# A row-sum stream on one core: two buffers of 24 rows in place of three of 16

## The chip, the core and the metric

The kernel runs on one core of a Trainium2 chip. The metric is the device time of one execution in microseconds (us); several runs are summarised by their median.

## The reference

```python
def setup_inputs():
    batch, seq, dim = 32, 512, 1024
    return {"x": np.random.randn(batch, seq, dim).astype(np.float32), "divisor": float(dim)}

def reference(x, divisor):
    return (np.sum(x, axis=-1) / divisor).astype(np.float32)
```

There are 16,384 rows of 1,024 float32 values. Each row is summed and divided by 1,024. The input has 67.1 MB, the output 64 KB.

## The kernel before, in words

Each of the 128 partitions is given J = 128 rows. They lie in three regions of `x`: the first F = 15 rows of each partition (`x_first`, where partitions are 15 rows apart), then M = 97 rows (`x_main`) and L = 16 rows (`x_last`), which share a region where partitions are W = M + L = 113 rows apart. The rows of one partition that one load fetches are contiguous in memory, so a load of 16 rows moves one run of 64 KB for each partition, 8 MB in all.

The loads go through three buffers, `bulk0` to `bulk2`, of 16 rows per partition each, used in turn. Their list is written by hand: from the main region 2 rows, five times 16, and 15; then the 15 rows of the first region; then two loads from the last region, of 10 rows and 640 elements and of 3 rows and 672 elements. Two small loads with places of their own (`pa`, `pb`) bring what is left of the last region, 1,344 and 416 elements per partition. The text counts the loads through the buffers from 0. Each buffer has a semaphore that its loads raise by 16 on landing.

All loads are issued by SP (SyncE) on one queue. The first two go out before anything else. The loop at L134 issues the others in order. Load 2 waits for load 0 to land. Each later load k waits until load k-3, which had the same buffer, has been reduced: `done_dve` and `done_act` hold the counts that the semaphores of DVE and ACT must reach. Behind the loop SP issues `pa` and `pb`, then the store of the first region's results (after POOL has scaled them), the store of the main region's, and last the store of `fin`, the results of the last region.

DVE (VectorE) takes one `reduce_sum` per load (L215). Of some loads it leaves the last rows to ACT, which sums a row per instruction (L183): the second number in each pair of the list says how many, 4 of the 15 in the last main load and 6 of the 15 in the first region's. POOL scales the results of these two regions (L157, L161). The rows of the last region are summed by DVE with an instruction that adds the two halves of a row (L205) and by ACT, both of which scale at once; the order of these is written so that little is left after the last bytes.

A change to the list of loads, to the number of buffers or to their size thus moves the landings, the reductions and the time at which SP may issue.

Of the kernel before, what the change touches and what calls it, by code (L numbers as in the profile page):

```python
# [35 lines left out]
def kernel(  # L36
# [6 lines left out]
    nc = tc.nc  # L43
    nc.at_finalize(start_loads_at_once)
    xf = x.flatten_outer_dims()
    N, D = xf.shape
# [2 lines left out]
    J = N // P  # L49
    assert J * P == N  # L50

    F, L = 15, 16
    M = J - F - L
    W = M + L
    x_first = bass.AP(tensor=x.tensor, offset=0, ap=[[F * D, P], [1, F * D]])
# [1 line left out]
    x_last = bass.AP(tensor=x.tensor, offset=P * F * D + M * D, ap=[[W * D, P], [1, L * D]])  # L57
# [4 lines left out]
    def room(name, *shape):  # L62
        return nc.alloc_sbuf_tensor(name, [P, *shape], F32).ap()
# [2 lines left out]
    base = -(-nc.sbuf_base // 32) * 32  # L66
    room("pad", -base % 1024 // 4)
    assert nc.sbuf_base % 1024 == 0
    bulk = [room(f"bulk{i}", 16 * D) for i in range(3)]

# [2 lines left out]
    ends = [0, 10 * D + c10, 14 * D + c14, 15 * D + c15, 16 * D]  # L75
# [11 lines left out]
    loads = []  # L87
    sems = {}

    def sem(name):  # L90
        sems[name] = nc.alloc_semaphore(name)
        return sems[name]

    in_bulk = [sem(f"in_bulk{i}") for i in range(3)]
    in_pa, in_pb = (sem(f"in_{n}") for n in ("pa", "pb"))
    out_first, out_main = sem("out_first"), sem("out_main")
    dve, act, pool = sem("by_dve"), sem("by_act"), sem("by_pool")
    done = sem("done")
    landed = nc.alloc_semaphore("landed")

    main = [(2, 0)] + [(16, 0)] * 5 + [(15, 4)]
    first = [(15, 6)]
    assert sum(r for r, _ in first) == F and sum(r for r, _ in main) == M
    for rows_of, src, dst in ((main, x_main, res), (first, x_first, res0)):
        j = 0
        for rows, on_act in rows_of:
            t = bulk[len(loads) % 3][:, : rows * D]
            loads.append((t, in_bulk[len(loads) % 3], src[:, j * D : (j + rows) * D], on_act, dst[:, j : j + rows]))
            j += rows
    for k in range(2):  # L110
        t = bulk[len(loads) % 3][:, : ends[k + 1] - ends[k]]
        loads.append((t, in_bulk[len(loads) % 3], x_last[:, ends[k] : ends[k + 1]], 0, None))


    for t, s, src, *_ in loads[:2]:
        i = nc.sync.dma_start(out=t, in_=src).then_inc(s, 16)
        tc.no_tile_sem_insts.add(i.ins.name)
    tc.close()
    tc.compile()  # L119
# [2 lines left out]
    done_dve, done_act = {}, {}  # L122
# [4 lines left out]
    arrived, seen = [], {}  # L127
# [6 lines left out]
    for k, (t, s, src, *_) in enumerate(loads):  # L134
        if k < 2:
            continue
        if k == 2:
            nc.sync.wait_ge(loads[0][1], arrived[0])
        else:
            nc.sync.wait_ge(dve, done_dve[k - 3])  # L140
            if done_act[k - 3]:
                nc.sync.wait_ge(act, done_act[k - 3])
            nc.sync.wait_ge(s, arrived[k] - 16)
        nc.sync.dma_start(out=t, in_=src).then_inc(s, 16)
    nc.sync.dma_start(out=pa, in_=x_last[:, ends[2] : ends[3]]).then_inc(in_pa, 16)
    nc.sync.dma_start(out=pb[:, : D - c15], in_=x_last[:, ends[3] : ends[4]]).then_inc(in_pb, 16)
    nc.sync.wait_ge(pool, 3)
# [6 lines left out]
    k = len(main) - 1  # L154
# [31 lines left out]
    for k, (t, s, src, on_act, dst) in enumerate(loads[:-2]):  # L186
        rows = t.shape[1] // D
# [23 lines left out]
    for k, (t, s, src, on_act, dst) in enumerate(loads[:-2]):  # L211
        m = t.shape[1] // D - on_act
        nc.vector.wait_ge(s, arrived[k])
        rows = t[:, : m * D].rearrange("p (r d) -> p r d", d=D)
# [65 lines left out]
```

## Time and profile before

| | us |
|---|---|
| median of 3 runs | 160.44 |
| lowest, highest | 160.27, 160.67 |
| span of the profiled execution, from its first to its last instruction | 159.3 |
| DVE busy in it | 116.7 |
| ACT busy in it | 18.6 |
| a 16-row reduction on DVE | 17.22 |
| a row on ACT | 1.01, and 0.19 to read the sum |

The page gives the span as the profiled execution's own time; the median of the unprofiled runs lies 1.1 us above it, which is the time around the first and last instruction. The DMA queue moved 67.18 MB in 2,160 packets, at 422 GB/s over the span. The time from issue to landing of a load (a median of 40.8 us for the 16-row loads) includes its wait behind earlier loads in the queue.

A line of the timeline has the start and the duration in us, the engine, the line of the kernel, the operation, what it writes and reads, and in brackets the idle time of the engine ahead of it and what ended that. Landing means that the load's semaphore is full. "SPq" is SP's instruction queue, which issues the DMAs.

### The profile page before, as it was taken

What the parts mean: (1) busy time and instruction counts of PE and PEld (TensorE: products, weight loads), DVE (VectorE), ACT (ScalarE), POOL (GpSimd) and SP (SyncE); (2) the same over time, 40 slices, a digit from 0 to 9 for tenths busy, and PEclk for the clock granted to TensorE, in tenths of its full rate; (3) what the DMA queues carried; (4) which work ended last, traced back from release to release, by engine and by line L of the source; (5) the groups of instructions that cost most, each with busy time, mean ns of one, the idle gap of its engine ahead of it and who ended that gap; (6) DMA issues with size and microseconds to landing.
All of it is one profiled execution on the core that took longest, in us unless ns stands there. A gap on an engine that the chain in (4) does not pass through costs nothing.

```text
span 159.3 us, 144 instructions
## 1 busy us (share of the span) xinstructions
DVE 116.7 (73%) x32; ACT 18.6 (12%) x35; POOL 1.0 (1%) x7
## 2 busy tenths in 40 slices
DVE  0500009999499994999949999499989990399296
ACT  3000000000000000000000000000009100392196
POOL 0000000000000000000000000000000001000000
DMA  8996996996996997979969969969996999889894
GB/s 296 494 527 263 527 527 263 527 527 263 527 527 263 527 444 346 527 313 477 527 263 527 527 263 527 494 278 463 494 494 262 478 494 494 350 350 525 344 401 154
DMA packets 2160, 67.18 MB, mean 422 GB/s; under 512 B 624, under 2 KB 752, under 8 KB 880
## 3 DMA queue, kind: packets, MB, share of 16 engines
q1 hardware_dynamic: 2160, 67.18, 98.1%
HBM read 67.11 MB, written 0.07 MB: 422 GB/s over the span
## 4 chain that ended last, share of the span: by engine, by line
DMA 67%; DVE 30%; another core or an unknown queue 1%; issue 0%
DMA bulk<-in_x_dram 67%; DVE res L215 29%; DVE bulk L205 1%; DVE tail L205 0%; DVE pb L205 0%; DVE fin L205 0%
## 5 line engine op out<-in xcount | busy, mean ns | idle before, releaser
L215 DVE TENSOR_REDUCE res<-bulk 128x16 f32<-128x16384 f32 (+3 forms) x8 | 110.0, 13754 | 37.7 <-DMA bulk<-in_x_dram 37.7
L183 ACT ACTIVATE junk<-bulk 128x1024 f32<-128x1024 f32 (+1 forms) x16 | 15.6, 973 | 137.2 <-DMA bulk<-in_x_dram 137.2
L205 DVE CUSTOM_DVE_ANT_0 bulk<-bulk 128x512 f32<-128x512 f32 (+1 forms) x9 | 5.5, 665 | 3.1 <-DMA bulk<-in_x_dram 3.1
L183 ACT ACTIVATION_READ_ACCUMULATOR junk<-bulk 128x1 f32 x16 | 3.0, 187 | 0.0
L183 ACT ACT_TABLE_LOAD x1 | 1.3, 1283 | 1.9 <-PEq L119 1.9
L157 POOL TENSOR_SCALAR res<-res 128x97 f32<-128x97 f32 x1 | 0.5, 465 | 129.8 <-DVE res L215 129.8
L205 DVE DVE_READ_ACCUMULATOR2_ANT fin<- 128x1 f32 x10 | 0.8, 82 | 0.0
L183 ACT ACTIVATE junk<-tail 128x737 f32<-128x737 f32 x1 | 0.8, 789 | 0.0
L205 DVE CUSTOM_DVE_ANT_0 bulk<-bulk,part 128x192 f32<-128x192 f32 x1 | 0.4, 420 | 0.3 <-DMA bulk<-in_x_dram 0.3
L205 DVE CUSTOM_DVE_ANT_0 tail<-tail 128x304 f32<-128x304 f32 x1 | 0.5, 476 | 0.0
L205 DVE CUSTOM_DVE_ANT_0 pb<-pb 128x209 f32<-128x209 f32 x1 | 0.4, 379 | 0.1
L161 POOL TENSOR_SCALAR res<-res 128x15 f32<-128x15 f32 x1 | 0.3, 262 | 15.6 <-DVE res L215 15.6
L183 ACT ACTIVATION_READ_ACCUMULATOR junk<-tail 128x1 f32 x1 | 0.2, 187 | 0.0
L153 POOL MEMSET pb<- 128x2 f32 x1 | 0.1, 99 | 1.5 <-POOLq L119 1.5
L261 POOL MEMSET const-bfloat16-1.0<- 128x1 bf16 x1 | 0.1, 101 | 0.0
L261 POOL MEMSET const-uint8-127<- 128x1 uint8 x1 | 0.1, 101 | 0.0
L261 POOL MEMSET const-float32-0.0<- 128x1 f32 x1 | 0.1, 98 | 0.2 <-issue 0.2
L261 POOL MEMSET const-float32-1.0<- 128x1 f32 x1 | 0.1, 98 | 0.0
L205 DVE DVE_READ_ACCUMULATOR2_ANT pb<- 128x1 f32 x1 | 0.1, 84 | 0.0
L205 DVE DVE_READ_ACCUMULATOR2_ANT part<- 128x1 f32 x1 | 0.1, 83 | 0.0
## 6 DMA issues: line engine op xcount, KB each, us to landing
bulk<-in_x_dram SPq DMA_DIRECT2D x2, 7680.0 KB, 39.3
bulk<-in_x_dram SPq DMA_DIRECT2D x1, 5440.0 KB, 32.0
bulk<-in_x_dram SPq DMA_DIRECT2D x1, 1872.0 KB, 23.5
bulk<-in_x_dram SPq DMA_DIRECT2D x1, 1024.0 KB, 4.6
tail<-in_x_dram SPq DMA_DIRECT2D x1, 672.0 KB, 24.7
pb<-in_x_dram SPq DMA_DIRECT2D x1, 208.0 KB, 24.8
bulk<-in_x_dram SPq DMA_DIRECT2D x5, 40.8
out_dram<-res SPq DMA_DIRECT2D x1, 48.5 KB, 1.6
```

Of the source, the lines that this page charges most:

```text
L153: nc.gpsimd.memset(pb[:, D - c15 :], 0.0).then_inc(pool)
L157: nc.gpsimd.tensor_scalar_mul(out=res, in0=res, scalar1=scale).then_inc(pool)
L161: nc.gpsimd.tensor_scalar_mul(out=res0, in0=res0, scalar1=scale).then_inc(pool)
L183: nc.scalar.activation(scratch, src, COPY, scale=by, accum_out=dst).then_inc(count)
L205: return nc.vector.tensor_tensor_reduce(out=src[:, :h], in0=src[:, :h], in1=src[:, h:], scale=by, scalar=ahead, op0=ADD, op1=ADD, accum_ou ...
L215: nc.vector.reduce_sum(out=dst[:, :m], in_=rows, axis=AX).then_inc(dve)
L261: nc = _bacc.Bacc("TRN2", target_bir_lowering=False, num_devices=1)
```

## The change

The three buffers of 16 rows become two of 24, which take the same room (192 KB per partition). The main region has 98 rows in loads of 2 and four times 24, with 8 rows of the last of them left to ACT; the first region has 14 rows, 5 of them on ACT; the last region's 16 rows, their loads and their arithmetic are as before. Partitions of the main and last regions lie 114 rows apart. A load of 24 rows is written as two runs of 12 rows (48 KB) per partition. Load k now waits for load k-2 to be reduced, and load 2 does so as well, where it waited for load 0's landing. There are eight loads through the buffers (0 to 7) in place of ten (0 to 9): load 4 is the last of the main region, load 5 the first region, loads 6 and 7 the last one.

```diff
-    F, L = 15, 16
+    F, L = 14, 16
...
-    bulk = [room(f"bulk{i}", 16 * D) for i in range(3)]
+    bulk = [room(f"bulk{i}", 24 * D) for i in range(2)]
...
-    in_bulk = [sem(f"in_bulk{i}") for i in range(3)]
+    in_bulk = [sem(f"in_bulk{i}") for i in range(2)]
...
-    main = [(2, 0)] + [(16, 0)] * 5 + [(15, 4)]
-    first = [(15, 6)]
+    main = [(2, 0)] + [(24, 0)] * 3 + [(24, 8)]
+    first = [(14, 5)]
...
-            t = bulk[len(loads) % 3][:, : rows * D]
-            loads.append((t, in_bulk[len(loads) % 3], src[:, j * D : (j + rows) * D], on_act, dst[:, j : j + rows]))
+            t = bulk[len(loads) % 2][:, : rows * D]
+            loads.append((t, in_bulk[len(loads) % 2], src[:, j * D : (j + rows) * D], on_act, dst[:, j : j + rows]))
...
-        t = bulk[len(loads) % 3][:, : ends[k + 1] - ends[k]]
-        loads.append((t, in_bulk[len(loads) % 3], x_last[:, ends[k] : ends[k + 1]], 0, None))
+        t = bulk[len(loads) % 2][:, : ends[k + 1] - ends[k]]
+        loads.append((t, in_bulk[len(loads) % 2], x_last[:, ends[k] : ends[k + 1]], 0, None))
...
+    def load(t, src):
+        if t.shape[1] > 16 * D:
+            t, src = (v.rearrange("p (c f) -> p c f", c=2) for v in (t, src))
+        return nc.sync.dma_start(out=t, in_=src)
...
-        if k == 2:
-            nc.sync.wait_ge(loads[0][1], arrived[0])
-        else:
-            nc.sync.wait_ge(dve, done_dve[k - 3])
-            if done_act[k - 3]:
-                nc.sync.wait_ge(act, done_act[k - 3])
-            nc.sync.wait_ge(s, arrived[k] - 16)
-        nc.sync.dma_start(out=t, in_=src).then_inc(s, 16)
+        nc.sync.wait_ge(dve, done_dve[k - 2])
+        if done_act[k - 2]:
+            nc.sync.wait_ge(act, done_act[k - 2])
+        nc.sync.wait_ge(s, arrived[k] - 16)
+        load(t, src).then_inc(s, 16)
```

More of the change, by code (lines that the diff above doesn't have):

```diff
@@ L106 @@
         for rows, on_act in rows_of:
-            t = bulk[len(loads) % 3][:, : rows * D]
-            loads.append((t, in_bulk[len(loads) % 3], src[:, j * D : (j + rows) * D], on_act, dst[:, j : j + rows]))
+            t = bulk[len(loads) % 2][:, : rows * D]
+            loads.append((t, in_bulk[len(loads) % 2], src[:, j * D : (j + rows) * D], on_act, dst[:, j : j + rows]))
             j += rows
     for k in range(2):
-        t = bulk[len(loads) % 3][:, : ends[k + 1] - ends[k]]
-        loads.append((t, in_bulk[len(loads) % 3], x_last[:, ends[k] : ends[k + 1]], 0, None))
+        t = bulk[len(loads) % 2][:, : ends[k + 1] - ends[k]]
[4 more added lines that the diff above has]
+        return nc.sync.dma_start(out=t, in_=src)
     for t, s, src, *_ in loads[:2]:
-        i = nc.sync.dma_start(out=t, in_=src).then_inc(s, 16)
+        i = load(t, src).then_inc(s, 16)
         tc.no_tile_sem_insts.add(i.ins.name)
```

## The prediction

> **What bounds the kernel now.** I read the page's totals first, then the timeline of DVE and of SP's issues, then the stretches in which the DMA engines fall idle, and the instruction groups by shape for prices.
>
> The totals:
>
> ```profile
> span 159.3 us, 144 instructions
> ...
> DVE 116.7 (73%) x32; ACT 18.6 (12%) x35; POOL 1.0 (1%) x7
> ...
> q1 hardware_dynamic: 2160, 67.18, 98.1%
> ```
>
> The one DMA queue has packets in flight on the 16 engines for 98.1% of the span; DVE, the busiest engine, works for 73%. So the stream of loads sets the time, and compute matters in two ways only: the tail after the last byte, and the moment at which a buffer comes free for the next load. The timeline gives both (start, duration, line, operation, and in brackets the idle time before):
>
> ```profile
> 43.28 17.22 DVE L215 TENSOR_REDUCE res<-bulk 128x16 f32<-128x16384 f32 x1 [2.13 <-DMA bulk<-in_x_dram]
> 62.65 17.22 DVE L215 TENSOR_REDUCE res<-bulk 128x16 f32<-128x16384 f32 x1 [2.15 <-DMA bulk<-in_x_dram]
> ...
> 119.83 11.89 DVE L215 TENSOR_REDUCE res<-bulk 128x11 f32<-128x11264 f32 x1 [1.04 <-DMA bulk<-in_x_dram]
> ...
> 137.99 9.76 DVE L215 TENSOR_REDUCE res<-bulk 128x9 f32<-128x9216 f32 x1 [6.26 <-DMA bulk<-in_x_dram]
> ...
> 150.82 0.49 DVE L205 CUSTOM_DVE_ANT_0 bulk<-bulk 128x320 f32<-128x320 f32 x1 [3.08 <-DMA bulk<-in_x_dram]
> ```
>
> Each reduction starts some 0.02 us after its load has landed, so starts are landings. A 16-row load takes 62.65 - 43.28 = 19.37 us; from the first start (4.61) to that of the fourth 16-row load (81.98) 64 rows take 77.37, which is **1.209 us a row**. DVE needs 17.22 for the same 16 rows and waits 2.1 at each seam. SP's issue of the buffer that has come free, from its own timeline:
>
> ```profile
> 60.53 0.33 SPq L144 DMA_DIRECT2D bulk<-in_x_dram  x1
> ```
>
> At 60.53 one load has 2.1 us left, a whole further load is queued behind it, and this one goes behind both. With three buffers the stream has over 21 us of work ahead whenever SP issues; it cannot run dry.
>
> **The change part by part.**
>
> *DVE's price for other row counts.* The groups by shape:
>
> ```profile
> L215 DVE TENSOR_REDUCE res<-bulk 128x16 f32<-128x16384 f32 x5 | 86.1, 17220 | 25.8 <-DMA bulk<-in_x_dram 25.8
> ...
> L215 DVE TENSOR_REDUCE res<-bulk 128x9 f32<-128x9216 f32 x1 | 9.8, 9755 | 6.3 <-DMA bulk<-in_x_dram 6.3
> ...
> L215 DVE TENSOR_REDUCE res<-bulk 128x2 f32<-128x2048 f32 x1 | 2.3, 2286 | 4.6 <-DMA bulk<-in_x_dram 4.6
> ```
>
> (17.220 - 2.286) / 14 = 1.067 us a row and 0.153 fixed; this gives 9.755 for nine rows, as measured. So 24 rows cost 25.76, and DVE's 16 rows of the last main load 17.22. ACT's eight rows there cost 8 x 1.04 = 8.4 (its 1.01 us ACTIVATEs start 1.04 apart), beside DVE and done 9 us earlier.
>
> *Bytes and packets.* The rows are the same 128. In the packet records a 65,536-byte packet starts 2.4145 us after the one before it on its engine, and a 61,440-byte one 2.2635: both 0.1509 a row, so two 48 KB packets in place of one cost nothing measurable. Two fewer loads remove two completion packets, 0.006 us each on an engine. Sum: 0.
>
> *The start.* Load 0 (2 rows) is alike. The third load now waits for DVE's 2-row reduction and goes at 4.61 + 2.29 = 6.9 instead of 4.60; load 1 (24 rows) covers it until 33.6. What is queued behind that wait on SP is only later loads. Cost 0; without that cover it would be 2.3.
>
> *The 24-row seams.* Now load k+2 is issued when load k is reduced, with only the rest of load k+1 ahead of it. A 24-row load takes 29.0, its predecessor's reduction 25.76: SP issues 3.2 us before the running load lands (loads 3, 4 and 5, at about 59.4, 88.4 and 117.4, against landings at 62.6, 91.6 and 120.6). By the packet records engines finish 0.34 to 0.7 us before the landing, so some 2.5 us are left for the issue to bring its first packet. What that takes, the stretches beside an idle queue show (share of the DMA engines, GB/s in the last two columns):
>
> ```profile
> 0.00:0.90 0.90, 0.00 (x0) 0.00 (x0) 0.19 (x4) 1.00 0.00 0
> 0.90:1.00 0.10, 0.00 (x0) 0.00 (x0) 0.00 (x0) 1.00 0.41 82
> ...
> 158.60:158.70 0.10, 0.00 (x0) 0.00 (x0) 0.00 (x0) 1.00 0.08 9
> ```
>
> The first load, issued at 0.00, has its first packet just before 1.00; the last store, issued at 157.85, at 158.68. So 0.83 to 1.0, against 2.5: hidden, cost 0.
>
> *The seam before the last region.* Here the cover fails. Load 6 (10.6 rows of the last 16) takes the buffer of load 4, which DVE works on for 17.22 from its landing. Ahead of it there is only load 5, the first part, 14 rows long: 14 x 1.209 = 16.93. Load 4 lands at 4.61 + 96 x 1.209 = 120.7 and load 5 at 137.6; DVE is done with load 4 at 137.9, and SP issues load 6 at 137.93 (0.03 after DVE's end, as at 41.15 and 41.18). That is **0.33 after load 5 has landed**: the DMA engines are dry, and every later byte of the stream is late by the gap. Three buffers had this load queued at 118.82, 19 us early.
>
> The gap's size: load 6 lands an empty-queue overhead plus its transfer time after its issue, where before it landed its transfer time after load 5. So the loss is 0.33 plus that overhead. The trace has two rows on an empty queue. The last store (8 KB) lands 1.4 us after its issue, under 0.1 of it packets: 1.3 or more of overhead, a loss of 1.65. Load 0 lands 4.58 after its issue; less 2 x 1.209 that is 2.16, a loss of 2.49. Load 0 is the nearer row, since it is a read of the same tensor, but its first packets took 0.3 to 0.8 us where later ones of that size took 0.309, with a second load issued 0.43 behind it and all engines starting together. I expect part of that slow start and take an overhead of 1.77: **a loss of 2.1**, ends 1.65 and 2.5.
>
> The Trainium skill ("DMA: Bandwidth & Descriptors", section on the anatomy of one DMA) fits a transfer alone as about 2.0 us plus bytes over 436 GB/s, on the GpSimd path; by that estimate load 6 (5.57 MB) needs 14.8 against 12.84 in the trace, a loss of 2.3 rather than 2.1.
>
> *After it.* Load 7 waits for load 5's reduction (nine rows, 137.9 + 9.76 = 147.7, issue then; the two small loads follow on SP by 148.6), and load 6's data run until about 152.3, so the queue stays fed. From load 6's landing on, loads and instructions are those of before: 159.3 - 150.8 = 8.5 us. POOL's scalings and the first store come at 148, idle work.
>
> Sum on the profiled execution: 159.3 + 2.1 = 161.4 of span. The median lies 1.1 above the span (160.44 against 159.3); I keep that: **162.5 us**.
>
> **The rivals.**
>
> 1. *Two buffers suffice* (no change, 160.4). If load 6 were issued 1.3 us before load 5's landing there would be no gap. That needs DVE's 16 rows to take 15.6 where five of them took 17.22 on average. Chance 0.03. The Trainium skill ("Trainium Kernel Development and Optimization", Best Practices) advises double buffering to overlap DMA with compute, and would make this the case; no row here shows a two-deep queue.
>
> 2. *A fixed cost per load, and two loads fewer* (faster). If each load paid the last store's 1.4 on the stream, two fewer would bring -2.8, and with the gap +2.1 the time is 159.7. It decides from 1.05 us per load up. Against it: eight 65,536-byte packets per engine take 8 x 2.4145 = 19.32, and the first four landings are 19.32 to 19.37 apart, so a seam costs under 0.05. Chance 0.03. The fixed 2.0 us named above, if it held per queued DMA, would give -4.0 here; the trace disagrees.
>
> 3. *The 24-row seams fail too* (slower still). A load in two runs a partition is 256 descriptors; nothing in the trace is issued so. Should its first packet need three times the 0.83 to 1.0, it comes up to 0.5 late at loads 3 and 4 (load 5 has one run again): +1.0, 163.5; it decides above 2.5 us. For it: an engine stretched now and then (the fifth 16-row landing came 0.25 late) eats cover. Chance 0.07.
>
> 4. *Slower reads at the new pitch.* 114 rows instead of 113 lie between partitions' reads. The only bad stretch shown, 19.6 for 16 rows instead of 19.35, is 1.3%; over 114 rows 1.8 us, 164.3 with the gap. Against it: undisturbed 61,440-byte packets take 2.267 at the 15-row and at the 113-row pitch alike. Chance 0.03.
>
> A view folded back into one run per partition would leave the last gap as it is, since load 6 has one run anyway.
>
> **How the numbers follow.** The forecast, one gap before the last region, has 0.84. Its own range is 1.65 to 2.5 plus 0.3 either way for stretched packets: 161.8 to 163.2. Reaching to rival 3 (163.5, and some above) gives 161.7 to 163.8, leaving out rivals 1, 2, 4. A measurement of this kernel can tell about 0.3%, 0.5 us, from no change. Faster 0.03 (rival 2), same 0.03 (rival 1), slower 0.94.
>
> **What would show it right or wrong.** Right: DVE's 24-row reductions at 25.8 each, SP's issues about 3.2 before the landings up to load 5; load 6 issued some 0.3 after load 5's landing, next to DVE's end of the 16-row reduction; a stretch of some 1.5 us near 138 without DMA; load 6 landing near 15 us after load 5 instead of 12.8; 8.5 from there to the end. Wrong: no idle DMA at 138 (rivals 1, 2), landings of 24 rows over 29.3 apart with the DMA engines idle at 62 and 91 (rival 3) or with packets over 1.82 us each (rival 4).

## The result and the profile after

The changed kernel takes 164.34 us (median of 5 runs, 163.88 to 164.98) against 160.44: a ratio of 1.0244, 95% interval 1.0232 to 1.0257. That is 3.9 us slower; 2.1 was forecast, and the range ended at 163.8. A later series gave 1.0263 (1.0245 to 1.0282). Ratios, here and below, leave out a run that lay over 1.5% above the fastest of its kernel; two of the experiments had one each. The span of the profiled execution grew from 159.3 to 163.0, 3.7 us.

The totals after:

```profile
span 163.0 us, 145 instructions
...
DVE 113.2 (69%) x30; ACT 21.8 (13%) x41; POOL 1.0 (1%) x7
...
q1 hardware_dynamic: 2384, 67.18, 96.7%
```

The same bytes are moved, but packets are in flight for less of the span, so the time went into a stream that is not fed. DVE's timeline shows where (start, duration, line, operation, idle time before):

```profile
4.82 2.29 DVE L217 TENSOR_REDUCE res<-bulk 128x2 f32<-128x2048 f32 x1 [4.82 <-DMA bulk<-in_x_dram]
33.77 25.75 DVE L217 TENSOR_REDUCE res<-bulk 128x24 f32<-128x24576 f32 x1 [26.67 <-DMA bulk<-in_x_dram]
62.76 25.75 DVE L217 TENSOR_REDUCE res<-bulk 128x24 f32<-128x24576 f32 x1 [3.24 <-DMA bulk<-in_x_dram]
92.00 25.75 DVE L217 TENSOR_REDUCE res<-bulk 128x24 f32<-128x24576 f32 x1 [3.48 <-DMA bulk<-in_x_dram]
...
121.92 17.22 DVE L217 TENSOR_REDUCE res<-bulk 128x16 f32<-128x16384 f32 x1 [4.17 <-DMA bulk<-in_x_dram]
...
139.32 9.75 DVE L217 TENSOR_REDUCE res<-bulk 128x9 f32<-128x9216 f32 x1 [0.19 <-DMA bulk<-in_x_dram]
...
154.49 0.49 DVE L207 CUSTOM_DVE_ANT_0 bulk<-bulk 128x320 f32<-128x320 f32 x1 [5.42 <-DMA bulk<-in_x_dram]
```

The reductions cost what was worked out (25.75 for 24 rows). The landings do not keep their distance: 28.99 from load 1 to load 2, then 29.24 and 29.92 to loads 3 and 4. Load 4 lands at 121.9 instead of 120.7. The next lines are from SP's timeline: the issue of load 5 and of load 6. Behind them stand the stretches around the last issue (columns: stretch, length, busy times of DVE, ACT and POOL, clock, share of the DMA engines, GB/s):

```profile
117.78 0.34 SPq L118 DMA_DIRECT2D bulk<-in_x_dram  x1
...
139.16 0.34 SPq L118 DMA_DIRECT2D bulk<-in_x_dram  x1
```

```profile
136.00:137.00 1.00, 1.00 (x1) 0.00 (x0) 0.00 (x0) 1.00 0.79 344
137.00:137.30 0.30, 0.30 (x1) 0.00 (x0) 0.00 (x0) 1.00 0.00 0
137.30:139.10 1.80, 1.80 (x1) 0.00 (x0) 0.00 (x0) 1.00 0.01 0
```

A packet is counted in the stretch in which it starts, so 0.00 alone is not idleness; the packet records complete it. The engines finish load 5 between 137.5 and 139.0, and load 6 has its first packets at 140.1 to 141.0, so all 16 engines stand still, each for a time between 1.1 and 3.5 us. Load 6 lands 15.3 us after its issue, where its bytes alone take 12.84.

So the forecast gap is there, but it is not the whole loss: the seams between the 24-row loads, costed at nothing, lose time too.

### The profile page after: what moved, and what is told of

Read it like the earlier page. It is cut to its first block, busy times and chain, and to the rows that moved or that the text cites. A ratio compares the mean times of both kernels' runs of the same rounds, so it can differ in the third digit from the quotient of the medians.

```text
span 163.0 us, 145 instructions
## 1 busy us (share of the span) xinstructions
DVE 113.2 (69%) x30; ACT 21.8 (13%) x41; POOL 1.0 (1%) x7
## 4 chain that ended last, share of the span: by engine, by line
DMA 60%; DVE 38%; ACT 1%; issue 1%; SPq 0%
DMA bulk<-in_x_dram 60%; DVE res L217 38%; ACT junk L185 1%; SPq L118 0%
## 5 line engine op out<-in xcount | busy, mean ns | idle before, releaser
L217 DVE TENSOR_REDUCE res<-bulk 128x24 f32<-128x24576 f32 (+3 forms) x6 | 106.5, 17753 | 42.6 <-DMA bulk<-in_x_dram 42.6
L185 ACT ACTIVATE junk<-bulk 128x1024 f32<-128x1024 f32 (+1 forms) x19 | 18.6, 978 | 137.8 <-DMA bulk<-in_x_dram 137.8
L185 ACT ACTIVATION_READ_ACCUMULATOR junk<-bulk 128x1 f32 x19 | 3.5, 187 | 0.0
L159 POOL TENSOR_SCALAR res<-res 128x98 f32<-128x98 f32 x1 | 0.5, 466 | 137.2 <-DVE res L217 137.2
## 6 DMA issues: line engine op xcount, KB each, us to landing
bulk<-in_x_dram SPq DMA_DIRECT2D x1, 5440.0 KB, 15.3
```

Source lines behind the costliest of these rows:

```text
L159: nc.gpsimd.tensor_scalar_mul(out=res, in0=res, scalar1=scale).then_inc(pool)
L185: nc.scalar.activation(scratch, src, COPY, scale=by, accum_out=dst).then_inc(count)
L217: nc.vector.reduce_sum(out=dst[:, :m], in_=rows, axis=AX).then_inc(dve)
```

## Experiments

Below, a load's *lead* is the time from SP's issue of it to the landing of the load ahead of it in the queue. It depends on how many rows DVE keeps: each row given to ACT frees the buffer 1.07 us earlier. In the changed kernel loads 3, 4 and 5 have a lead of 3.2 to 4.1, load 6 of 0.14 and load 7 of 5.4; in the kernel before, the 16-row loads have over 21.

*Theory A:* an issue on a busy stream takes more than the lead to bring all engines their first packets, so some engines run dry, and first packets are stretched. *Rival B:* the form of the loads (two runs per partition) or the new spacing of 114 rows unbalances the engines, whatever the lead. Ratios are to the kernel before on the same chip; "above before" is the ratio applied to the median of before there (160.36 to 160.56).

### Only the last seam closed

```diff
-    main = [(2, 0)] + [(24, 0)] * 3 + [(24, 8)]
+    main = [(2, 0)] + [(24, 0)] * 3 + [(24, 12)]
```

> The changed kernel with ACT taking 12 rows of load 4 instead of 8, so DVE reduces 12 rows (12.95 us) and load 6 is issued about 4 us before load 5 lands instead of 0.14 before it. The prediction's step (the gap before load 6 is the whole loss): about 160.5. Theory A (a load issued only 2 to 3 us ahead of its turn also has its first packets stretched on some engines, here at loads 3, 4 and 5): the gap of 2.3 goes and the rest stays, 161.5 to 162.3. Rival B (the two-run form or the new pitch unbalances the engines): the same 161.5 to 162.3; this run only prices the gap.

Measured: ratio 1.0113 (1.0091 to 1.0136), 1.8 us above before. The gap's removal gives back about 2.1, and nearly as much stays: the gap is not the whole loss. The rest is not the seams alone, though. With load 6 in time, load 7 is issued only 3.1 us before load 6 lands, and in the profile it lands 0.45 late; the next run shows this more strongly. This does not tell A from B.

### Every load early, still two buffers of 24 rows in two runs

```diff
-    main = [(2, 0)] + [(24, 0)] * 3 + [(24, 8)]
+    main = [(2, 0)] + [(24, 6)] * 3 + [(24, 12)]
```

> The changed kernel with ACT taking 6 rows of loads 1 to 3 and 12 of load 4, so that every load is issued 9 us (load 6: 4 us) ahead of the landing of the load before it. Two buffers, 24 rows, two runs and pitch as in the changed kernel. Theory A (late issues stretch first packets): all loss goes, 160.2 to 160.8, landings 29.0 apart, no stretched packets at the seams. Rival B (form or pitch): the seams stay stretched, 161.5 to 162.3.

Measured: 1.0107 (1.0086 to 1.0128), 1.7 above before. That is the time that rival B gave, but not by its way: it had the seams stay stretched, and in the profile loads 0 to 6 are in time (load 6 lands at 150.8, as in the kernel before). The loss lies at load 7, which theory A had not counted. That load has a lead of 3.0 there, since the DVE part of load 5 holds its buffer:

```profile
147.80 0.33 SPq L118 DMA_DIRECT2D bulk<-in_x_dram  x1
```

Packets at its start are stretched by up to 0.99 us, and load 7 lands at 156.25 instead of 155.3. The trouble had moved to the one load whose lead was still 3 us. The next run gives that load a lead as well:

```diff
-    first = [(14, 5)]
+    first = [(14, 7)]
```

> As e2_share, and ACT also takes 7 rows of load 5 instead of 5, so that load 7 is issued 5.2 us before load 6 lands (3.0 in e2_share). Every load is now issued at least 4 us ahead. Theory A (issues 2 to 3 us ahead are late, since the first packets come 2.2 to 3.8 us after the issue when the engines are busy): 160.3 to 160.8, no stretched packets at load 7. Rival B (form or pitch): as e2_share, 161.7 to 162.2.

Measured: 160.91, 1.0021 (1.0012 to 1.0030). Of the 3.9 us, 0.35 are left (theory A's range ended at 160.8, and the kernel before takes 160.56 on this chip). Nothing but the shares of DVE and ACT was changed: two buffers, 24 rows, two runs per partition and the spacing are those of the changed kernel. Rival B falls as the cause of the loss.

```profile
62.92 19.35 DVE L217 TENSOR_REDUCE res<-bulk 128x18 f32<-128x18432 f32 x1 [9.65 <-DMA bulk<-in_x_dram]
92.00 19.35 DVE L217 TENSOR_REDUCE res<-bulk 128x18 f32<-128x18432 f32 x1 [9.72 <-DMA bulk<-in_x_dram]
120.97 12.95 DVE L217 TENSOR_REDUCE res<-bulk 128x12 f32<-128x12288 f32 x1 [9.62 <-DMA bulk<-in_x_dram]
```

Landings are 29.08 and 28.97 apart, as the bytes demand.

### The two terms, each alone, on top of that version

The seams (`main` with `[(24, 0)] * 3 + [(24, 12)]`, `first` with `(14, 7)`):

> As e5_all, but loads 1 to 3 are all on DVE as in the changed kernel: loads 3, 4 and 5 are issued 3.2 us before the running load lands, loads 6 and 7 in good time. The prediction's zero for these seams: the time of e5_all within 0.3. Theory A: 0.4 to 1.5 above it, with stretched packets at the starts of loads 3 to 5 and the 16 engines' ends apart by up to 1.5 us.

The gap (`[(24, 6)] * 3 + [(24, 8)]`, `(14, 7)`):

> As e5_all, but ACT takes 8 rows of load 4 as in the changed kernel: only load 6 is late, issued about 0.3 us after load 5 has landed. The prediction's gap alone: 1.65 to 2.5 above e5_all, 2.1 taken. Theory A: the engines are idle then, first packets 1.0 to 1.9 us after the issue as in the changed kernel's profile, then slow ones: 2.2 to 2.6 above e5_all. If both hold, the rest of the changed kernel's loss lies at the other loads.

Measured: seams 162.88, 1.0140 (1.0126 to 1.0155), so **2.0 above** the version with all loads early (theory A had 0.4 to 1.5); gap 163.48, 1.0180 (1.0166 to 1.0194), **2.6 above** it. The seams in DVE's timeline:

```profile
62.98 25.75 DVE L217 TENSOR_REDUCE res<-bulk 128x24 f32<-128x24576 f32 x1 [3.24 <-DMA bulk<-in_x_dram]
92.93 25.75 DVE L217 TENSOR_REDUCE res<-bulk 128x24 f32<-128x24576 f32 x1 [4.19 <-DMA bulk<-in_x_dram]
121.91 12.95 DVE L217 TENSOR_REDUCE res<-bulk 128x12 f32<-128x12288 f32 x1 [3.23 <-DMA bulk<-in_x_dram]
```

Load 3 lands 0.95 late (29.95 after load 2). The packet records, paired by their times, show one engine without a packet from 62.37 to 63.09, and packets at this seam stretched by up to 0.9 us. Thirteen engines end load 3 by 91.7, three at 92.2 to 92.6, and it lands at 92.9: a few late engines out of 16 are enough. The next seam, where load 4 has a lead of 4.1 because load 3 landed late, loses nothing. Against the version with all loads early, some 0.35 are lost at load 5 and as much at load 7.

The two terms do not add: 2.0 and 2.6 on top of 0.35 make 4.9, and the changed kernel lost 3.9 and 4.2. The profiles show one overlap. Load 6 is issued when DVE is done with load 4, 17.2 us after that load has landed. A load 5 that is late at its own seam lands later, and so covers more of that wait: in the two profiles of the changed kernel it lands 17.40 and 18.07 after load 4, and load 6 is issued 0.14 and 0.81 before that landing. In the gap's run it lands 17.23 after load 4, and load 6 is issued 0.04 behind it. Whether this is the whole difference was not tried.

How much lead is enough, with one row of loads 1 to 3 on ACT:

> As e8_seam0 with one row of loads 1 to 3 on ACT, so that loads 3, 4 and 5 are issued 4.3 us before the running load lands (3.2 in e8_seam0, 9.6 in e5_all). Theory A, from the 2.2 to 3.8 us that first packets took on busy engines, and 0.4 to 0.7 between an engine's end and the landing: within 0.5 above e5_all, against 2.0 in e8_seam0.

Measured: 160.92, 1.0028 (1.0018 to 1.0038). With 1.07 us more lead at three seams the 2.0 us are gone:

```profile
62.80 24.69 DVE L217 TENSOR_REDUCE res<-bulk 128x23 f32<-128x23552 f32 x1 [4.30 <-DMA bulk<-in_x_dram]
91.87 24.69 DVE L217 TENSOR_REDUCE res<-bulk 128x23 f32<-128x23552 f32 x1 [4.39 <-DMA bulk<-in_x_dram]
120.88 12.95 DVE L217 TENSOR_REDUCE res<-bulk 128x12 f32<-128x12288 f32 x1 [4.33 <-DMA bulk<-in_x_dram]
```

The landings are 29.07 and 29.01 apart. DVE reads each load for nearly as long as in the seams' run (24.69 and 25.75), so its reading is not what slows the stream. A lead of 3.2 can cost and one of 4.3 does not. It need not cost each time: in the run with only the last seam closed, loads 3 and 4 have a lead of 3.2 too, and in its profile they land 29.07 and 28.98 after the load ahead.

### An issue on busy engines

```diff
-    main = [(2, 0)] + [(24, 6)] * 3 + [(24, 8)]
+    main = [(2, 0)] + [(24, 6)] * 3 + [(24, 10)]
```

> As e6_gap8 with 10 rows of load 4 on ACT: load 6 is issued about 1.8 us before load 5 lands, so while the engines are busy. By the prediction's 0.83 to 1.0 us from issue to first packet: no gap, the time of e5_all within 0.3. Theory A (2.2 to 3.8 us on busy engines): 0.7 to 2.3 above e5_all, so issuing 2.1 us earlier than in e6_gap8 gains far less than 2.1.

Measured: 162.98, 1.0154 (1.0139 to 1.0169), 2.1 above the version with all loads early. Issued 2.3 us earlier than in the gap's run, load 6 wins 0.5:

```profile
138.13 7.62 DVE L217 TENSOR_REDUCE res<-bulk 128x7 f32<-128x7168 f32 x1 [2.16 <-DMA bulk<-in_x_dram]
152.84 0.49 DVE L207 CUSTOM_DVE_ANT_0 bulk<-bulk 128x320 f32<-128x320 f32 x1 [7.09 <-DMA bulk<-in_x_dram]
```

Load 6 is issued at 136.00, the engines finish load 5 from 137.1 on, and the last engine has its first packet of load 6 at 139.05, **3.05 us after the issue**; first packets are stretched by up to 0.96. In the gap's run, where the engines stood idle at the issue (138.30), first packets came after 0.96 to 1.85. The 0.83 to 1.0 of the prediction is thus right for the first engine on an idle queue, and not for the last one, idle or busy.

Two runs were to show whether an engine must first finish the large packet that it has begun. The first wrote load 5 as seven runs of 2 rows:

```diff
+        if t.shape[1] == 14 * D:
+            t, src = (v.rearrange("p (c f) -> p c f", c=7) for v in (t, src))
```

> As e7_gap10 (load 6 issued 1.8 us before load 5 lands), but load 5 is written as seven runs of 2 rows (8 KB) per partition, so that 8 KB packets of 0.31 us instead of 56 KB packets of 2.12 us are in flight when SP issues load 6. If an issue on a busy queue is slow because the engine finishes the large packets that it has begun (theory A1): first packets about 1 us after the issue, the time within 0.5 of e5_all plus 0.2 for the small packets. If the delay does not hang on the packets in flight (theory A2, for example the descriptors' own way to the engines): as e7_gap10, 2.1 above e5_all.

Measured: 162.52, 1.0138 (1.0122 to 1.0155). But its packet records still have 57,344-byte packets: adjoining runs that fit into one packet were folded back into one. It is a repeat of the run before it, 2.2 above before against 2.5. The second made load 5 of seven separate DMAs, and their packets stayed apart:

```diff
+        for c in range(parts[k]):
+            n = t.shape[1] // parts[k]
+            load(t[:, c * n : (c + 1) * n], src[:, c * n : (c + 1) * n]).then_inc(s, 16)
```

> As e7_gap10 (load 6 issued 1.8 us before load 5 lands), but load 5 is made of seven DMAs of 2 rows each, all issued in good time, so that the packets in flight when SP issues load 6 have 8 KB (0.31 us) and not 56 KB (2.12 us). Theory A1 (an engine gets to the new descriptors only behind the large packet it has begun): first packets of load 6 about 1 to 1.9 us after the issue, at or just after the engines' ends, so 0.3 to 1.0 above e5_all's place (0.35 above before, so 0.7 to 1.4 above before). Theory A2 (the delay does not hang on the packets in flight): as e7_gap10 and e9_small, 2.1 to 2.4 above before.

Measured: 162.50, 1.0135 (1.0110 to 1.0160), 2.2 above before, with 8 KB packets of 0.31 us in flight. First packets of load 6 still come up to 2.3 us after the issue, and are stretched by up to 0.6.

```profile
138.25 7.62 DVE L220 TENSOR_REDUCE res<-bulk 128x7 f32<-128x7168 f32 x1 [2.25 <-DMA bulk<-in_x_dram]
152.30 0.49 DVE L210 CUSTOM_DVE_ANT_0 bulk<-bulk 128x320 f32<-128x320 f32 x1 [6.43 <-DMA bulk<-in_x_dram]
```

From load 5 to load 6 the landings are 14.05 apart, against 14.71 and 14.50 in the two runs with large packets, and 12.84 when issued early. Of the 1.66 to 1.87 that the late issue adds there, 1.21 are left with small packets in flight, and in the measured time no gain is seen (2.2 above before, against 2.5 and 2.2). The packet in flight is at most a third of the delay by these single profiles; A1 as the main cause falls.

### Depth two with 16-row loads, and the form alone

The kernel before with two buffers, `len(loads) % 2`, and the waits on `k - 2`; nothing else changed:

> The kernel before with two buffers of 16 rows instead of three, all else alike: loads 3 to 6 are issued 2.1 us before the running load lands, with one run per partition and the old pitch, and there is no gap at the end (load 8 goes 6 us ahead). The prediction's cost of zero for seams (0.83 to 1.0 to the first packet against some 1.5 left): 160.4 to 160.7. Theory A: five seams of 0.2 to 0.8 each, 161.5 to 163. Rival B: 160.4 to 160.7.

Measured: 166.76, 1.0417 (1.0393 to 1.0441), 6.7 above before: more than any forecast. In the profile the leads of loads 3 to 6 are 2.1, 2.5, 2.4 and 4.1, that of load 7, which goes behind a load of only 15 rows, is 1.3, and that of the last load, 9, is 3.0. The landings of loads 4 and 5, and the issue of load 7:

```profile
82.78 17.22 DVE L212 TENSOR_REDUCE res<-bulk 128x16 f32<-128x16384 f32 x1 [2.44 <-DMA bulk<-in_x_dram]
104.17 17.22 DVE L212 TENSOR_REDUCE res<-bulk 128x16 f32<-128x16384 f32 x1 [4.17 <-DMA bulk<-in_x_dram]
```

```profile
121.41 0.33 SPq L141 DMA_DIRECT2D bulk<-in_x_dram  x1
```

A load that lands late (104.1, 21.4 after the one before it, for 19.35 us of bytes) is reduced late, and so the issue that hangs on it is late for the engines that had finished early: at 121.41 several had been dry since 120.8. I had priced the seams singly and left out that the engines drift apart and one delay can feed the next. I had also left out load 9: it lands 6.0 after load 8, against 4.5 in the kernel before, so about 1.6 of the loss lie there and not at the seams between 16-row loads.

The same two buffers with 5 rows of each main load and 8 of the first region's on ACT:

> As e3_depth2 (two buffers of 16 rows, old pitch and regions), with 5 rows of every 16-row and 15-row main load and 8 rows of the first region's on ACT, so that each load is issued 5 to 7.5 us before the running load lands instead of 2.1. If only the late issue costs: 160.4 to 161.0, against 167.2 in e3_depth2. If a two-deep queue costs by itself: 162 or more.

Measured: 160.53, 1.0010 (1.0001 to 1.0018). A depth of two costs next to nothing by itself; the late issues cost 6.5 us.

The form alone, as it was meant:

> The kernel before with each 16-row load written as two runs of 8 rows (32 KB) per partition; three buffers, the same order and waits. Theory A: no change, 160.3 to 160.6. Rival B in its form part (two runs unbalance the engines): 161 to 162, with landings of the 16 engines spread over 0.6 us or more.

Measured: 160.33, 1.0000 (0.9991 to 1.0009). It says nothing on the form, since its packets have 65,536 bytes: these runs too had been folded. What speaks on the form is the version with all loads early, where the packets have 49,152.

### The changed kernel again, and what is left

> The changed kernel again, on the chip of these runs. Gap (2.6 in e6_gap8) and seams (2.0 in e8_seam0) above e5_all would add to 4.5 if they were independent; 3.9 above the kernel before was measured, so I expect 3.5 to 4.0 above before, and engines whose ends at load 5 are apart by over 1 us.

Measured: 164.77, 1.0263 (1.0245 to 1.0282), 4.2 above before, a little over what was expected. In this profile the engines end load 5 between 137.1 and 139.5, and two engines have no packet for 0.6 and 0.9 us at the seam near 62.3.

For the 0.35 that the version with all loads early keeps over the kernel before, the pitch was tried, with the old regions (15 rows, 113 rows apart):

```diff
-    F, L = 14, 16
+    F, L = 15, 16
...
-    main = [(2, 0)] + [(24, 6)] * 3 + [(24, 12)]
-    first = [(14, 7)]
+    main = [(2, 0)] + [(24, 6)] * 3 + [(23, 11)]
+    first = [(15, 8)]
```

> As e5_all with the regions of the kernel before (first part 15 rows, 113 rows between partitions): the last main load has 23 rows, 11 of them on ACT, load 5 has 15 rows, 8 of them on ACT, so all issues stay at least 5 us ahead. e5_all is 0.35 above before. If that is the pitch (load 0 landed 0.2 to 0.4 later in every profile at 114 rows): within 0.1 of before. If it is the two-deep queue or the 24-row loads: 0.3 to 0.4 above before.

Measured: 160.66, 1.0020 (1.0011 to 1.0030), the same ratio as at the new spacing. Load 0 does land sooner (4.54 against 4.93 in the profiles), but the time does not follow. The last 0.3 us stay open. No version tried beats the kernel before.

## Why the prediction was wrong

Added up again step by step, the prediction's own terms give a span of 161.0 (load 6 issued at 137.93, landing 14.61 later, 8.5 to the end; the 161.4 of the text carried 0.4 of stretched packets from the old profile). Measured was 163.0. The 2.0 lie in three terms. A further 0.2 is the step from span to median: 1.1 was taken, and the runs that list both times have 1.3 (163.0 and 164.34 here).

- **Seams at zero: wrong, and the step that failed.** "What that takes, the stretches beside an idle queue show ... So 0.83 to 1.0, against 2.5: hidden, cost 0." The price was read from the first packet of the first engine on an idle queue. What a seam needs is the first packet of the last of 16 engines on a busy stream. In the run with load 6 issued 1.8 us ahead that took 3.05 us, and slow packets came after it. In the changed profile the 96 rows up to load 4 took 117.1 instead of 116.1, 1.04 us; alone, with the gap closed, the seams cost 2.0. Rival 3 had the right place and a threshold that fits (it decides above 2.5 us) but the wrong reason: it hung on 256 descriptors, while one-run loads (5, 6 and 7, and all in the 16-row test) are late in the same way. It had 0.07.
- **The gap: right in place, too small.** SP issued load 6 0.02 after DVE's end, 0.14 before load 5's landing, with the engines dry. Its overhead is 15.31 - 12.84 = 2.47 instead of 1.77, 0.70 more: the row of load 0 (2.16) was nearer than the middle that was taken. Alone the gap costs 2.6, just above the upper end of 2.5. The Trainium skill's fit ("DMA: Bandwidth & Descriptors", anatomy of one DMA), 14.8 for this load, was nearer too, and still short of the 15.3 here.
- **The start at zero: 0.2 off.** Load 0 landed at 4.8 instead of 4.6, and at 4.8 to 5.0 in all other profiles with 114 rows between partitions, against 4.5 to 4.7 with 113. That is all that is seen of rival 4, and a spacing of 113 did not bring the time down.
- **Right:** DVE's and ACT's prices, the packets' price (1,024 packets of 48 KB at 1.815 us in the version with all loads early), load 7 and the small loads, and 8.5 us from load 6's landing to the end.
- **Rival 1** ("two buffers suffice") was ruled out here by DVE's 17.22, but is true once SP issues early: 1.0010 and 1.0021. The Trainium skill's advice to double-buffer ("Trainium Kernel Development and Optimization", Best Practices) holds in this case only with that condition, which that line does not state. **Rival 2** (a fixed cost per load) is refuted: ten DMAs of loads instead of twelve brought nothing, in any version.

## What to carry to other kernels

In a stream bound by DMA, a free buffer is not enough: the next load must be issued early enough that every engine can begin it when it finishes the load before. Here a lead of 3.2 us cost between nothing and 0.95 us at a seam, one of 4.3 cost nothing, and the lead was bought by moving single rows from the reducing engine to an idle one. Lead counted to the landing overstates what the engines that finish first have, since the last engine sets the landing. With a queue only two deep a late landing delays the next issue, so the losses can feed each other: 6.7 us where the first leads were 2.1 to 2.5.

## What the runs showed of the hardware that was not expected

- Issue to first packet is a spread over the engines: 0.96 to 1.85 us with idle engines, up to 3.05 with busy ones; with 8 KB packets in flight still up to 2.3. Why a busy stream slows it stays open.
- First packets of a late load are slow themselves: up to 1.2 us over the usual 2.1 for 57,344 bytes at the start of load 5 in the changed profile. Most loads with a lead of 4 us or more had at most 0.5, but a lead counted to the landing does not protect when the engines have drifted apart. That load 5 had a lead of 4.1, load 6 of the run with two buffers of 16 rows had 4.1 and a first packet stretched by 0.95, load 7 of the seams' run had 5.2 and 1.0. In all three the engines ended the load ahead 1.3 to 2.0 us apart, so the first of them was free 2.5, 1.8 and 3.2 us after the issue.
- Adjoining runs of a load were folded into one packet where they fit into 64 KB: views of 2 x 32 KB and 7 x 8 KB came out as 65,536 and 57,344 bytes, 2 x 48 KB stayed two.
